# First token half four slabs ahead, table loads on SyncE: one change to a decoder trunk on one core

## The chip, the cores and the metric

The kernel runs on one core of a Trainium2 chip. It has TensorE (PE in the profile; its weight loads are PEld), VectorE (DVE), ScalarE (ACT), GpSimd (POOL) and SyncE (SP, which only starts transfers here). The metric is the device time of one execution in microseconds, as the median of several runs.

## The reference

A trunk of two post-norm layers over 256 tokens of 2048 channels in fp32. Every layer does `h = LN(a*h + mixer(h))`, then `h = LN(a*h + ffn(h))`.

```python
def reference(x, ...):
    for layer in range(DEPTH):                      # DEPTH = 2
        if layer % 2 == 0:
            mix = even_mixer(...)   # Mamba-2 SSD (16 heads) and block attention (8 heads)
        else:
            mix = odd_mixer(...)    # NSA (compressed, selected, window) and retention
        h = layer_norm(DEEPNORM_ALPHA * h + mix, ln_g[layer, 0], ln_b[layer, 0])
        ffn = conv_ffn(h, ffn_w_up[layer], ffn_conv_w[layer], ffn_conv_b[layer], ffn_w_down[layer])
        h = layer_norm(DEEPNORM_ALPHA * h + ffn, ln_g[layer, 1], ln_b[layer, 1])
def conv_ffn(x, w_up, conv_w, conv_b, w_down):
    a, u = jnp.split(x @ w_up, 2, axis=-1)
    return (jax.nn.silu(causal_depthwise_conv(a, conv_w, conv_b)) * u) @ w_down
```

Attention adds a relative-position bias, a table of 32 buckets by 8 heads. The SSD needs `dt = softplus(dt_raw + dt_bias)` before its decays.

## The kernel before

**Precision and the weight stream.** Each fp32 operand is split into a high half (rounded to the matmul's type) and a low half (the rest), and a product is made of three matmuls: high x high, high x low, low x high. All weights, some 430 MB, come once from HBM in slabs of up to 128x1024. SyncE loads a slab into `wraw` (L103), ScalarE rounds it to `whi` (L115), VectorE subtracts to `wlo` (L116); each has four buffers. `pump` splits slabs ahead of their use, `limit` bounds how far, `load` only starts transfers. With `pin` an instruction keeps its place in the program's order; the rest are ordered by the Tile scheduler when the kernel is built. On each engine the order is fixed from then on, and an engine stands at an instruction until what it needs is there.

**Jobs.** A projection is one of several kinds of jobs: `group_b` leaves channels on partitions (weights stationary, L267 and in the head L219 and L223), `group_a` and `group_t` leave tokens on partitions (`products`, L307 to L309). Tokens are two halves of 128, t = 0 and 1.

**The four LayerNorms.** `out_proj` (idx 0 to 3) makes the last projection of each half layer in four column groups of 512. In the last one the final slabs (`skew`) run first for t = 0, then for t = 1, so that the first token half ends earlier. VectorE adds it to the residual r, makes statistics (`bn_stats`, `bn_aggr`, `rs`), GpSimd raises `rs` to the power -1/2, VectorE centres the first 512 channels. `late` then calls `norm(idx, 0)`: TensorE transposes the first `SPLIT` channel blocks, ScalarE makes of each the high half `x` (L434) and the plain value y (L435, in a spare `wraw`), and VectorE the low half (`lows`, L437).

**Junctions.** After idx 0, 1 and 2 the next job begins with `SPLIT` head slabs, one channel block each (`head_slabs`): first all for t = 0, then all for t = 1. Ahead of the last one of t = 0 `ready` calls `norm(idx, 1)`, which does the same for the second token half. The other channel blocks follow, two at a time, in `norm_full`. I call these junctions 0, 1 and 2. Junctions 0 and 2 lead into an up-projection (`group_b`; `head_b` uses high weights alone for t = 0, and both high and low for t = 1). Junction 1 leads into the odd layer's `group_a` job, whose head uses high and low weights for both halves.

**The tables.** `load_bias` brings the bias, two heads at a time, from a scratch in HBM (`scr`) into `tmp` (two buffers, shared with the sums of `group_b`'s halves, L345 and L348), and VectorE copies it reversed into `nb` (L568). The even layer also loads a causal `mask`. Before, GpSimd issues these, pinned, in program order. At that place VectorE makes the softplus as a chain of small operations (L758 to L771), then `neg` (L774), which TensorE needs at L779.

Of the kernel before, what the change touches and what calls it, by code (L numbers as in the profile page):

```python
# [9 lines left out]
F32 = mybir.dt.float32  # L10
F32R = mybir.dt.float32r
AF = mybir.ActivationFunctionType
OP = mybir.AluOpType
# [5 lines left out]
KT = DM // 128  # L19
# [6 lines left out]
BIG = 1e30  # L26
NCMP = 15
AHEAD = 3
SPLIT = 3

EV_Z, EV_XS, EV_B, EV_C, EV_DT, EV_Q, EV_K, EV_V = 0, 1024, 2048, 2304, 2560, 2576, 3600, 4624
OD_Q, OD_KC, OD_VC, OD_KS, OD_VS, OD_KW, OD_VW, OD_G, OD_RQ, OD_RK, OD_RV, OD_RG = (
# [48 lines left out]
class Weights:  # L81
# [21 lines left out]
            self.nc.sync.dma_start(raw[:, :z], bass.AP(tensor=ap.tensor, offset=ap.offset + off, ap=[[z, 128], [1, z]]))  # L103
            self.raw.append(raw)

    def prep(self, i, pin=False):
        nc = self.nc
        ap, off, kind, m, width = self.slabs[i]
        n = m * width
        if not self.raw:  # L110
            self.load(i + 1)
        raw = self.raw.pop(0)
        hi = self.pool.tile([128, 1024], F32R, name="whi", bufs=4)
        lo = self.pool.tile([128, 1024], F32R, name="wlo", bufs=4)
        a = nc.scalar.activation(hi[:, :n], raw[:, :n], AF.Copy)  # L115
        b = nc.vector.tensor_tensor(lo[:, :n], raw[:, :n], hi[:, :n].bitcast(F32), op=OP.subtract)  # L116
        if pin:
            self.tc.keep_in_program_order(a)
            self.tc.keep_in_program_order(b)
        self.ready[i] = (hi[:, :n].rearrange("p (k c) -> p k c", k=m), lo[:, :n].rearrange("p (k c) -> p k c", k=m))  # L120

    def pump(self, n, pin=False):
        while self.done < min(n, len(self.slabs)):
            self.prep(self.done, pin)
            self.done += 1

    def get(self, i):
        self.pump(max(i + 1, min(i + AHEAD + 1, self.limit)))
# [39 lines left out]
class Trunk:  # L168
# [22 lines left out]
    def head_slabs(self, first, half):  # L191

        w = self.w
        n, ready = self.head
        self.head = None
        slabs = [w.get(first + i) for i in range(n)]
        for t in range(2):
            for k, (hi, lo) in enumerate(slabs):
                if t == 0 and k == n - 1:
                    ready()  # L200
                    w.pump(first + n + 1, pin=True)
                half(t, k, hi[:, 0], lo[:, 0])
                if t == 1:
                    self.apply_to(n + k + 1)
                    self.fill.pop()
        w.limit = len(w.slabs)
        return n
# [103 lines left out]
    def group_t(self, act, accs, evac, drain=None, skew=1, late=None):  # L311

        w = self.w
        first = w.first[self.job]
        self.job += 1
        m = w.slabs[first][3]  # L320
        n = act.shape[1] // m
        runs = [[s] for s in range(n - skew)] + [list(range(n - skew, n))]
        for run in runs:
            if run[0] == drain:
                self.fill.flush()
            slabs = [w.get(first + s) for s in run]
            for t in range(2):
                for s, (hi, lo) in zip(run, slabs):
                    for kk in range(m):
                        if late and t == 1 and s == n - 1 and kk == m - 1:  # L330
                            late()
                        self.products(accs[t], act, m * s + kk, t, hi[:, kk], lo[:, kk])
                        if t == 1:
                            self.fill.pop()
                if run[-1] == n - 1:
                    evac(accs[t], t)
# [16 lines left out]
    def out_proj(self, act, idx, rows=None):  # L353

        nc, r, w = self.nc, self.r, self.w
        bn = self.bn

        def evac(n):
            def go(acc, t):
                rg = r[:, t, 512 * n:512 * n + 512]  # L360
                add = nc.vector.tensor_tensor(rg, acc, rg, op=OP.add)
                if n == 3 and t == 1:
                    self.pin(add)
                    self.low()
                sums = nc.vector.bn_stats(bn[:, t, n, :], rg)
                if n < 3:
                    return
                self.pin(sums)
                self.stats(t)
                self.low()  # L370
                if idx < 3 and t == 0:
                    self.centre(0, 0, 512)
                elif idx < 3:
                    w.limit += 1
                    w.pump(w.limit, pin=True)
                else:
                    for c in range(0, DM, 512):
                        if t == 1 and c:
                            self.finish(0, c, rows)
                    for c in range(0, DM if t else 512, 512):  # L380
                        self.finish(t, c, rows)
            return go

        def late():
            self.norm(idx, 0)
            self.low()

        for n in range(4):
            if n % 2:
                accs = [self.ps() for _ in range(2)]  # L390
            else:
                accs = [self.acc_pool.tile([128, 2, 512], F32, name="acc")[:, 0, :] for _ in range(2)]
            if n == 3 and idx < 3:
                w.limit = w.first[self.job + 1] + SPLIT - 1
            self.group_t(act, accs, evac(n), drain=6 if n == 0 else None, skew=3 if n == 3 else 1,
                         late=late if n == 3 and idx < 3 else None)
        self.fill.flush()
        self.fill.rate = 1.0
        if idx < 3:
            self.applies = [(k, lambda k=k: self.norm_full(idx, k)) for k in (SPLIT, *range(SPLIT + 1, KT, 2))]  # L400
            self.head = SPLIT, lambda: self.norm(idx, 1)

    def pin(self, ins):
        return self.tc.keep_in_program_order(ins)
# [11 lines left out]
    def low(self):  # L416
        if self.lows:
            self.lows.pop(0)()

    def norm(self, idx, t):  # L420

        nc, r, x = self.nc, self.r, self.x
        if t == 0:
            self.scratch = self.w.pool.tile([128, 1024], F32, name="wraw", bufs=4)
        else:
            self.pin(self.centre(1, 0, 512))
        ps = self.ps()
        for k in range(SPLIT):
            nc.tensor.transpose(ps[:, 128 * k:128 * k + 128], r[:, t, 128 * k:128 * k + 128], self.ident)
        for k in range(SPLIT):  # L430
            g, b = self.lng[:, idx, k:k + 1], self.lnb[:, idx, k:k + 1]
            z, y = ps[:, 128 * k:128 * k + 128], self.scratch[:, 128 * (SPLIT * t + k):128 * (SPLIT * t + k) + 128]
            hi, lo = (x[:, k, 256 * i + 128 * t:256 * i + 128 * t + 128] for i in range(2))
            nc.scalar.activation(hi, z, AF.Identity, scale=g, bias=b)  # L434
            nc.scalar.activation(y, z, AF.Identity, scale=g, bias=b)  # L435
            self.lows.append(lambda lo=lo, y=y, hi=hi: self.pin(
                nc.vector.tensor_tensor(lo, y, hi.bitcast(F32), op=OP.subtract)))  # L437
        if t == 1:
            while self.lows:
                self.low()  # L440
            for half in range(2):
                self.pin(self.centre(half, 512, 512))

    def norm_full(self, idx, k0):

        nc, r, x = self.nc, self.r, self.x
        ks = [k0] if k0 == SPLIT else [k0, k0 + 1]
        ps = self.ps()
        for i, k in enumerate(ks):
            for t in range(2):  # L450
# [2 lines left out]
        for i, k in enumerate(ks):  # L453
            g, b = self.lng[:, idx, k:k + 1], self.lnb[:, idx, k:k + 1]
            z, y = ps[:, 256 * i:256 * i + 256], self.spare[:, 256 * (k % 4):256 * (k % 4) + 256]
            hi = x[:, k, :256]
# [102 lines left out]
    def load_bias(self, nb, tmp_pool):  # L559

        nc = self.nc
        self.nb = nb
        s = self.scr[:, :]
        for a in range(4):
            t = tmp_pool.tile([128, 2, 256], F32, name="tmp", bufs=2)
            self.pin(nc.gpsimd.dma_start(t, bass.AP(tensor=s.tensor, offset=s.offset + 2 * a * 384,
                                         ap=[[1, 128], [384, 2], [1, 256]])))
            nc.vector.tensor_copy(self.nb[:, 2 * a:2 * a + 2, :], t[:, :, ::-1])  # L568

    def softmax(self, P, S, nb0, nb1, w0, w1, z, stat, j):  # L570
# [94 lines left out]
    def even(self):  # L665
        nc, x = self.nc, self.x
        with ExitStack() as ctx:
            P = ctx.enter_context(self.tc.tile_pool(name="even", bufs=1))
            y = P.tile([128, KT, 512], F32R, name="y")
# [50 lines left out]
            self.zbufs = 3  # L720
            with self.tc.tile_pool(name="even2", bufs=1) as P2:
                mask = P2.tile([128, 384], F32, name="mask")
                self.pin(nc.gpsimd.dma_start(mask, self.I["c_mask"]))
                self.load_bias(P2.tile([128, H, 256], F32, name="nb"), P)
                self.fill.flush()
                self.fill.add(*self.ssd_steps(P2, y, dt, xs, bc, zs, mask))
# [4 lines left out]
                for i in range(4):  # L731
                    q = P2.tile([128, 2, 256], F32, name="q", bufs=2)
                    k = P2.tile([128, 2, 256], F32, name="k", bufs=2)
# [520 lines left out]
```

## Time and profile before

| what | value |
| --- | --- |
| median of 3 runs | 2327.4 us (2326.22 to 2328.61) |
| the profiled execution's own time | 2327.03 us |
| its span | 2325.3 us |
| TensorE busy | 2294.7 us, 99% |
| VectorE busy | 1442.3 us, 62% |
| ScalarE busy | 1133.3 us, 49% |
| GpSimd busy | 45.3 us, 2% |

The span is the time between the first and the last instruction of the profiled execution. TensorE does matmuls nearly all the time; the two engines that prepare its operands have half and a third of their time free, on average over stages that differ.

### The profile page before, as it was taken

How to read it: one execution, taken by the hardware profiler on the slowest of the kernel's cores; microseconds unless marked ns; L12 is line 12 of the kernel's file. 1: busy time of each engine (PE TensorE's matmuls, PEld its weight loads, DVE VectorE, ACT ScalarE, POOL GpSimd, SP SyncE). 2: the span in 40 equal slices, each digit the busy share in tenths (PEclk: the TensorE clock that was granted, in tenths of full speed). 3: DMA queues.
4: the chain of work that ended last, by engine and by line, in shares of the span. 5: the costliest groups of instructions: out<-in, count | busy, mean ns of one | idle time of the engine just before them, and what ended most of it. 6: DMA issues, size and time to landing. Idle time of an engine off the chain costs nothing.

```text
span 2325.3 us, 32033 instructions
## 1 busy us (share of the span) xinstructions
PE 2294.7 (99%) x12450; PEld 1975.9 (85%) x12450; DVE 1442.3 (62%) x2015; ACT 1133.3 (49%) x1501; POOL 45.3 (2%) x72
## 2 busy tenths in 40 slices
PE   8999999999999999999999999999999999999997
PEld 8888888888888888888789888888888888888885
DVE  5677656866666665444665667758766666654445
ACT  5544545655555554333545554437555555543342
POOL 0001000000000000000000000000000000000000
PEclk9999999999999999999999999999999999999998
DMA  8554444765556655666556634455655556566553
GB/s 287 193 171 154 163 166 158 228 197 189 188 190 188 191 187 192 192 193 195 183 194 221 227 109 146 154 180 191 217 190 190 189 185 189 190 222 198 194 192 125
DMA packets 124568, 436.62 MB, mean 188 GB/s; under 512 B 14176, under 2 KB 14480, under 8 KB 124288
## 3 DMA queue, kind: packets, MB, share of 16 engines
q1 hardware_dynamic: 120896, 422.58, 55.6%
q0 software_dynamic: 3520, 12.00, 1.9%
q8 instruction: 97, 1.59, 0.3%
q14 instruction: 55, 0.45, 0.1%
HBM read 432.41 MB, written 2.11 MB: 187 GB/s over the span
## 4 chain that ended last, share of the span: by engine, by line
PE 97%; DVE 1%; ACT 1%; DMA 1%; issue 0%; POOL 0%; SPq 0%; POOLq 0%; ACTq 0%; DVEq 0%
PE acc L267 57%; PE acc L308 7%; PE acc L307 7%; PE acc L309 7%; PE ps L309 5%; PE ps L307 5%; PE ps L308 5%; PE ps L659 1%; PE ps L267 1%; PE ps L598 0%; DMA tmp<-scr 0%; PE ps L451 0%; PE ps L625 0%; DVE wlo L116 0%; PE ps L597 0%
## 5 line engine op out<-in xcount | busy, mean ns | idle before, releaser
L116 DVE TENSOR_TENSOR wlo<-wraw,whi 128x1024 fp32r<-128x1024 f32 (+5 forms) x816 | 972.3, 1193 | 651.2 <-ACT whi L115 650.5
L115 ACT ACTIVATE whi<-wraw 128x1024 fp32r<-128x1024 f32 (+5 forms) x816 | 843.3, 1035 | 794.7 <-PE acc L267 288.9
L267 PE MATMUL acc<-x,whi 128*128 128x512 f32 x3816 | 1192.6, 398 | 0.0
L267 PEld LDWEIGHTS acc<-x,wlo 128*128 128x128 f32 x3816 | 700.7, 188 | 158.6 <-issue 0.2
L267 PE MATMUL acc<-x,wlo 128*128 128x256 f32 x3816 | 734.8, 279 | 0.0
L267 PEld LDWEIGHTS acc<-x,whi 128*128 128x128 f32 x3816 | 590.7, 189 | 12.5 <-issue 1.2
L345 ACT ACTIVATE tmp<-acc 128x512 f32<-128x512 f32 x120 | 71.6, 597 | 219.9 <-PE acc L267 217.3
L307 PE MATMUL ps<-whi,g 128*128 128x512 f32 x352 | 137.0, 389 | 0.0
L308 PE MATMUL acc<-wlo,g 128*128 128x512 f32 x352 | 137.0, 389 | 0.0
L309 PE MATMUL acc<-whi,g 128*128 128x512 f32 x352 | 137.0, 389 | 0.0
L308 PE MATMUL ps<-wlo,g 128*128 128x512 f32 x352 | 136.9, 389 | 0.0
L309 PE MATMUL ps<-whi,g 128*128 128x512 f32 x352 | 136.9, 389 | 0.0
L307 PE MATMUL acc<-whi,g 128*128 128x512 f32 x352 | 136.8, 390 | 0.0
L307 PE MATMUL acc<-whi,x 128*128 128x512 f32 (+4 forms) x288 | 101.1, 352 | 5.8 <-ACT whi L115 5.8
L308 PE MATMUL acc<-wlo,x 128*128 128x512 f32 (+4 forms) x288 | 100.7, 349 | 0.7 <-DVE wlo L116 0.7
L309 PE MATMUL acc<-whi,x 128*128 128x512 f32 (+4 forms) x288 | 100.1, 348 | 0.0
L307 PEld LDWEIGHTS acc<-whi,g 128*128 128x128 f32 x352 | 66.1, 188 | 14.2 <-DVE u L348 0.5
L309 PEld LDWEIGHTS acc<-whi,g 128*128 128x128 f32 x352 | 66.1, 188 | 13.8
L308 PEld LDWEIGHTS ps<-wlo,g 128*128 128x128 f32 x352 | 66.1, 188 | 13.7
L307 PEld LDWEIGHTS ps<-whi,g 128*128 128x128 f32 x352 | 66.1, 188 | 13.7
L309 PEld LDWEIGHTS ps<-whi,g 128*128 128x128 f32 x352 | 66.1, 188 | 13.7
L308 PEld LDWEIGHTS acc<-wlo,g 128*128 128x128 f32 x352 | 66.1, 188 | 13.6
(280 smaller groups left out, 1828.7 us busy)
## 6 DMA issues: line engine op xcount, KB each, us to landing
wraw<-in_up SPq DMA_DIRECT2D x328, 512.0 KB, 3.8
wraw<-in_down SPq DMA_DIRECT2D x176, 512.0 KB, 4.2
wraw<-in_od_in SPq DMA_DIRECT2D x96, 512.0 KB, 3.9
wraw<-in_ev_in SPq DMA_DIRECT2D x72, 512.0 KB, 3.6
wraw<-in_ev_out SPq DMA_DIRECT2D x32, 512.0 KB, 3.5
wraw<-in_od_out SPq DMA_DIRECT2D x32, 512.0 KB, 3.5
wraw<-in_up SPq DMA_DIRECT2D x32, 384.0 KB, 3.5
wraw<-in_ev_in SPq DMA_DIRECT2D x16, 344.0 KB, 4.4
```

The lines of the kernel that those rows point to most:

```text
L115: a = nc.scalar.activation(hi[:, :n], raw[:, :n], AF.Copy)
L116: b = nc.vector.tensor_tensor(lo[:, :n], raw[:, :n], hi[:, :n].bitcast(F32), op=OP.subtract)
L267: nc.tensor.matmul(acc, wt, mv, start=(k == 0 and i < len(unit)), stop=(k == nk - 1 and i >= len(unit)))
L307: nc.tensor.matmul(o, xh, wh, start=(k == 0), stop=False)
L308: nc.tensor.matmul(o, xh, wl, start=False, stop=False)
L309: nc.tensor.matmul(o, xl, wh, start=False, stop=(k == last))
L345: nc.scalar.activation(t, a[:, :, 256:], AF.Copy, scale=sign)
L659: nc.tensor.matmul(o[:, t * 128:(t + 1) * 128], a, b, start=(i == 0), stop=(i == len(mms) - 1))
```

## The change

- `SPLIT` becomes 4, 3, 4 for junctions 0, 1, 2; the last column group's `skew` is 4; the first half's transposes come one `kk` earlier.
- `prep` is parted: `prep_hi` does ScalarE's part and returns `rest`, VectorE's part. The last head slab is prepared in `norm(idx, 1)`, and its `rest` is called after all lows of the second half.
- For the first two blocks VectorE makes y itself, from PSUM (own name `own`), just ahead of the low.
- The mask and the four table loads go from GpSimd's queue, where they were pinned, to SyncE's, not pinned.

```diff
-SPLIT = 3
+SPLIT = (4, 3, 4)
...
-    def prep(self, i, pin=False):
+    def prep_hi(self, pin=False):
+        nc, i = self.nc, self.done
+        self.done += 1
...
         a = nc.scalar.activation(hi[:, :n], raw[:, :n], AF.Copy)
-        b = nc.vector.tensor_tensor(lo[:, :n], raw[:, :n], hi[:, :n].bitcast(F32), op=OP.subtract)
...
+        def rest():
+            b = nc.vector.tensor_tensor(lo[:, :n], raw[:, :n], hi[:, :n].bitcast(F32), op=OP.subtract)
+            if pin:
+                self.tc.keep_in_program_order(b)
+        return rest
     def pump(self, n, pin=False):
         while self.done < min(n, len(self.slabs)):
-            self.prep(self.done, pin)
-            self.done += 1
+            if not self.raw:
+                self.load(self.done + 1)
+            self.prep_hi(pin)()
...
-        slabs = [w.get(first + i) for i in range(n)]
+        slabs = [w.get(first + i) for i in range(n - 1)]
         for t in range(2):
-            for k, (hi, lo) in enumerate(slabs):
+            for k in range(n):
                 if t == 0 and k == n - 1:
+                    w.load(first + n)
                     ready()
-                    w.pump(first + n + 1, pin=True)
+                    w.limit = first + n + 1
+                    slabs.append(w.get(first + k))
+                hi, lo = slabs[k]
...
-                        if late and t == 1 and s == n - 1 and kk == m - 1:
+                        if late and t == 1 and s == n - 1 and kk == 0:
...
-                elif idx < 3:
-                    w.limit += 1
-                    w.pump(w.limit, pin=True)
-                else:
+                elif idx == 3:
...
         def late():
             self.norm(idx, 0)
             self.low()
+            self.low()
...
-            self.group_t(act, accs, evac(n), drain=6 if n == 0 else None, skew=3 if n == 3 else 1,
+            self.group_t(act, accs, evac(n), drain=6 if n == 0 else None, skew=4 if n == 3 else 1,
...
     def norm(self, idx, t):
+        n, w = SPLIT[idx], self.w
...
             self.pin(self.centre(1, 0, 512))
+            rest = w.prep_hi(pin=True)
...
-            nc.scalar.activation(hi, z, AF.Identity, scale=g, bias=b)
-            nc.scalar.activation(y, z, AF.Identity, scale=g, bias=b)
-            self.lows.append(lambda lo=lo, y=y, hi=hi: self.pin(
-                nc.vector.tensor_tensor(lo, y, hi.bitcast(F32), op=OP.subtract)))
+            self.pin(nc.scalar.activation(hi, z, AF.Identity, scale=g, bias=b))
+            if k >= 2:
+                self.pin(nc.scalar.activation(y, z, AF.Identity, scale=g, bias=b))
+            def low(lo=lo, y=y, hi=hi, z=z, g=g, b=b, own=k < 2):
+                if own:
+                    self.pin(nc.vector.tensor_scalar(y, z, g, b, op0=OP.mult, op1=OP.add))
+                self.pin(nc.vector.tensor_tensor(lo, y, hi.bitcast(F32), op=OP.subtract))
+            self.lows.append(low)
         if t == 1:
             while self.lows:
                 self.low()
+            rest()
             for half in range(2):
                 self.pin(self.centre(half, 512, 512))
...
-            self.pin(nc.gpsimd.dma_start(t, bass.AP(tensor=s.tensor, offset=s.offset + 2 * a * 384,
-                                         ap=[[1, 128], [384, 2], [1, 256]])))
+            nc.sync.dma_start(t, bass.AP(tensor=s.tensor, offset=s.offset + 2 * a * 384,
+                                         ap=[[1, 128], [384, 2], [1, 256]]))
...
-                self.pin(nc.gpsimd.dma_start(mask, self.I["c_mask"]))
+                nc.sync.dma_start(mask, self.I["c_mask"])
```

How the built order changes, at three places. Line numbers of the changed kernel are up to 16 higher than before's (L116 is L121, L437 is L450, L568 is L584).

Even layer, at the tables. GpSimd's rows of before:

```order
L723 DMA mask<-in_c_mask 128x384
L566 DMA tmp<-scr 128x2x256 x4
```

SyncE's rows of the changed kernel at that place (before, they were 72 weight loads in a row):

```order
L103 DMA wraw<-in_ev_in 128x1024 x31
L582 DMA tmp<-scr 128x2x256 x2
L103 DMA wraw<-in_ev_in 128x1024
L739 DMA mask<-in_c_mask 128x384
L103 DMA wraw<-in_ev_in 128x1024
L582 DMA tmp<-scr 128x2x256 x2
L103 DMA wraw<-in_ev_in 128x1024 x39
```

The first two table loads moved ahead of the mask, and the other two behind it, with one weight load each between.

Junction 1, VectorE. Before, from the second half's residual add (`r<-ps,r`) to the first lows of the second half (`x<-wraw,x` behind the centring `r<-r,mv,rs`):

```order
L361 TENSOR_TENSOR r<-ps,r 128x512
L437 TENSOR_TENSOR x<-wraw,x 128x128
L365 BN_STATS bn<-r 128x6
L408 BN_AGGR mv<-bn 128x2
L409 TENSOR_SCALAR rs<-mv 128x1
L437 TENSOR_TENSOR x<-wraw,x 128x128
L116 TENSOR_TENSOR wlo<-wraw,whi 128x1024
L414 TENSOR_SCALAR r<-r,mv,rs 128x512
L184 TENSOR_TENSOR y<-prm,y 128x16x2 x2
L437 TENSOR_TENSOR x<-wraw,x 128x128 x3
```

The changed kernel there, from the statistics on (`wraw<-ps,prm` is VectorE's own y, `x<-nb,x` a low of `norm_full`):

```order
L190 TENSOR_TENSOR y<-prm,y 128x16x2
L415 BN_AGGR mv<-bn 128x2
L416 TENSOR_SCALAR rs<-mv 128x1
L421 TENSOR_SCALAR r<-r,mv,rs 128x512
L449 TENSOR_SCALAR wraw<-ps,prm 128x128
L450 TENSOR_TENSOR x<-wraw,x 128x128
L449 TENSOR_SCALAR wraw<-ps,prm 128x128
L478 TENSOR_TENSOR x<-nb,x 128x256
L450 TENSOR_TENSOR x<-wraw,x 128x128 x2
L121 TENSOR_TENSOR wlo<-wraw,whi 128x1024
```

The third head slab's `wlo` moved from ahead of the centring to behind all lows of the second half and one of `norm_full`. On TensorE in the changed kernel the second half's transposes stand ahead of the first matmul that uses it:

```order
L316 MATMUL acc<-whi,x 128x512 x2
L438 MATMUL ps<-ident,r 128x128 x3
L467 MATMUL ps<-ident,r 128x128 x2
L317 MATMUL acc<-wlo,x 128x512
L318 MATMUL acc<-whi,x 128x512
```

The transposes of `norm_full` moved in front of that matmul as well; they stood behind it before.

Junction 0, VectorE. Before, from the first half's centring to its last low:

```order
L414 TENSOR_SCALAR r<-r,mv,rs 128x512
L116 TENSOR_TENSOR wlo<-wraw,whi 128x768
L437 TENSOR_TENSOR x<-wraw,x 128x128
L361 TENSOR_TENSOR r<-ps,r 128x512
L437 TENSOR_TENSOR x<-wraw,x 128x128
```

In the changed kernel:

```order
L421 TENSOR_SCALAR r<-r,mv,rs 128x512
L121 TENSOR_TENSOR wlo<-wraw,whi 128x768 x3
L449 TENSOR_SCALAR wraw<-ps,prm 128x128
L450 TENSOR_TENSOR x<-wraw,x 128x128
L449 TENSOR_SCALAR wraw<-ps,prm 128x128
L450 TENSOR_TENSOR x<-wraw,x 128x128
L370 TENSOR_TENSOR r<-ps,r 128x512
```

Two more splits stand between the centring and the first low, and two lows instead of one ahead of the second half's residual add.

## Rows read from the trace of the kernel before

**Rows 1.** Page, part 1: busy time, share of the span, instructions.
```profile
PE 2294.7 (99%) x12450; PEld 1975.9 (85%) x12450; DVE 1442.3 (62%) x2015; ACT 1133.3 (49%) x1501; POOL 45.3 (2%) x72
```

**Rows 2.** What TensorE waited for: us in total, times, longest us.
```profile
PE acc L219 <- DVE x L437: 3.9, 6, 1.0
PE ps L779 <- DVE neg L774: 3.1, 1, 3.1
PE acc L308 <- DVE wlo L116: 0.7, 2, 0.5
```

**Rows 3.** Timeline of GpSimd at the tables: start, duration, what, idle before.
```profile
129.35 1.45 POOL L566 DMA_DIRECT2D tmp<-scr  x2
134.97 1.61 POOL L566 DMA_DIRECT2D tmp<-scr  x2 [4.17 <-DMA tmp<-scr]
```

**Rows 4.** The table loads' line in the even layer, issue to landing.
```profile
DMA to landing us min/median/max: 3.5/4.7/4.9
```

**Rows 5.** Timeline of VectorE at the tables.
```profile
123.47 0.69 DVE L348 TENSOR_TENSOR pad<-acc,tmp 128x512 f32<-128x512 f32 x1 [1.29 <-ACT tmp L345]
...
127.93 1.22 DVE L116 TENSOR_TENSOR wlo<-wraw,whi 128x1024 fp32r<-128x1024 f32 x1
...
140.52 0.43 DVE L568 COPY nb<-tmp 128x512 f32<-128x512 f32 x1 [1.51 <-DMA tmp<-scr]
...
146.48 0.19 DVE L774 SCALAR_TENSOR_TENSOR neg<-dt,sp_a 128x32 f32<-128x32 f32 x1
```

**Rows 6.** Stretches behind that wait: busy by engine, PEclk, DMA share, GB/s.
```profile
148.40:151.90 3.50, 3.50 (x15) 3.17 (x15) 1.34 (x2) 0.00 (x0) 0.00 (x0) 0.51 0.80 254
151.90:156.00 4.10, 4.10 (x28) 3.66 (x28) 2.53 (x4) 2.55 (x4) 0.00 (x0) 1.00 0.10 41
```

**Rows 7.** Timeline of TensorE at junction 0.
```profile
383.96 0.74 PE L219 MATMUL acc<-x,whi 128*128 128x256 f32 x4 [0.52 <-DVE x L437]
...
386.14 0.71 PE L219 MATMUL acc<-x,whi 128*128 128x256 f32 x4 [0.41 <-DVE x L437]
...
387.39 0.55 PE L429 MATMUL ps<-ident,r 128*128 128x128 f32 x3 [0.30 <-DVE r L414]
...
389.16 0.51 PE L219 MATMUL acc<-x,whi 128*128 128x256 f32 x2 [1.00 <-DVE x L437]
```

**Rows 8.** Timeline of VectorE at junction 0.
```profile
382.05 0.95 DVE L116 TENSOR_TENSOR wlo<-wraw,whi 128x768 fp32r<-128x768 f32 x1
```

**Rows 9.** Groups by line and shape, VectorE, the SSD's masks from PSUM.
```profile
L816 DVE TENSOR_SCALAR L<-ps,acum 128x128 f32<-128x128 f32 x16 | 5.5, 341 | 0.0
```

**Rows 10.** Timeline of TensorE at junction 1.
```profile
1119.53 0.39 PE L307 MATMUL ps<-whi,g 128*128 128x512 f32 x1
...
1125.82 0.49 PE L429 MATMUL ps<-ident,r 128*128 128x128 f32 x3
...
1126.86 0.50 PE L307 MATMUL acc<-whi,x 128*128 128x512 f32 x1
```

**Rows 11.** Timeline of VectorE at junction 1.
```profile
1119.59 0.55 DVE L414 TENSOR_SCALAR r<-r,mv,rs 128x512 f32<-128x512 f32 x1 [0.68 <-POOL rs L410]
...
1121.83 0.68 DVE L361 TENSOR_TENSOR r<-ps,r 128x512 f32<-128x512 f32 x1
...
1123.65 0.15 DVE L409 TENSOR_SCALAR rs<-mv 128x1 f32<-128x1 f32 x1
...
1123.96 1.23 DVE L116 TENSOR_TENSOR wlo<-wraw,whi 128x1024 fp32r<-128x1024 f32 x1
...
1130.84 0.42 DVE L462 TENSOR_TENSOR x<-nb,x 128x256 fp32r<-128x256 f32 x1
```

**Rows 12.** Timeline of ScalarE at junction 1.
```profile
1122.85 1.08 ACT L115 ACTIVATE whi<-wraw 128x1024 fp32r<-128x1024 f32 x1
...
1126.35 0.46 ACT L434 ACTIVATE x<-ps,prm 128x128 fp32r<-128x128 f32 x1 [2.17 <-PE ps L429]
...
1129.81 0.60 ACT L459 ACTIVATE nb<-ps,prm 128x256 f32<-128x256 f32 x1
```

More of the change, by code (lines that the diff above doesn't have):

```diff
@@ L104, in load @@
             self.raw.append(raw)
-    def prep(self, i, pin=False):
-        nc = self.nc
+    def prep_hi(self, pin=False):
+        nc, i = self.nc, self.done
+        self.done += 1
         ap, off, kind, m, width = self.slabs[i]
         n = m * width
-        if not self.raw:
-            self.load(i + 1)
         raw = self.raw.pop(0)
@@ L115, in prep @@
         a = nc.scalar.activation(hi[:, :n], raw[:, :n], AF.Copy)
-        b = nc.vector.tensor_tensor(lo[:, :n], raw[:, :n], hi[:, :n].bitcast(F32), op=OP.subtract)
         if pin:
             self.tc.keep_in_program_order(a)
-            self.tc.keep_in_program_order(b)
         self.ready[i] = (hi[:, :n].rearrange("p (k c) -> p k c", k=m), lo[:, :n].rearrange("p (k c) -> p k c", k=m))
+        def rest():
[3 more added lines that the diff above has]
+        return rest
     def pump(self, n, pin=False):
         while self.done < min(n, len(self.slabs)):
-            self.prep(self.done, pin)
-            self.done += 1
+            if not self.raw:
+                self.load(self.done + 1)
+            self.prep_hi(pin)()
     def get(self, i):
@@ L393, in out_proj @@
             if n == 3 and idx < 3:
-                w.limit = w.first[self.job + 1] + SPLIT - 1
-            self.group_t(act, accs, evac(n), drain=6 if n == 0 else None, skew=3 if n == 3 else 1,
+                w.limit = w.first[self.job + 1] + SPLIT[idx] - 1
+            self.group_t(act, accs, evac(n), drain=6 if n == 0 else None, skew=4 if n == 3 else 1,
                          late=late if n == 3 and idx < 3 else None)
@@ L399, in out_proj @@
         if idx < 3:
-            self.applies = [(k, lambda k=k: self.norm_full(idx, k)) for k in (SPLIT, *range(SPLIT + 1, KT, 2))]
-            self.head = SPLIT, lambda: self.norm(idx, 1)
+            self.applies = [(k, lambda k=k: self.norm_full(idx, k)) for k in [3] * (SPLIT[idx] == 3) + list(range(4, KT, 2))]
+            self.head = SPLIT[idx], lambda: self.norm(idx, 1)
     def pin(self, ins):
@@ L422, in norm @@
         nc, r, x = self.nc, self.r, self.x
+        n, w = SPLIT[idx], self.w
         if t == 0:
-            self.scratch = self.w.pool.tile([128, 1024], F32, name="wraw", bufs=4)
+            self.scratch = w.pool.tile([128, 1024], F32, name="wraw", bufs=4)
         else:
             self.pin(self.centre(1, 0, 512))
+            rest = w.prep_hi(pin=True)
         ps = self.ps()
-        for k in range(SPLIT):
+        for k in range(n):
             nc.tensor.transpose(ps[:, 128 * k:128 * k + 128], r[:, t, 128 * k:128 * k + 128], self.ident)
-        for k in range(SPLIT):
+        for k in range(n):
             g, b = self.lng[:, idx, k:k + 1], self.lnb[:, idx, k:k + 1]
-            z, y = ps[:, 128 * k:128 * k + 128], self.scratch[:, 128 * (SPLIT * t + k):128 * (SPLIT * t + k) + 128]
+            z, y = ps[:, 128 * k:128 * k + 128], self.scratch[:, 128 * (n * t + k):128 * (n * t + k) + 128]
             hi, lo = (x[:, k, 256 * i + 128 * t:256 * i + 128 * t + 128] for i in range(2))
-            nc.scalar.activation(hi, z, AF.Identity, scale=g, bias=b)
-            nc.scalar.activation(y, z, AF.Identity, scale=g, bias=b)
-            self.lows.append(lambda lo=lo, y=y, hi=hi: self.pin(
-                nc.vector.tensor_tensor(lo, y, hi.bitcast(F32), op=OP.subtract)))
+            self.pin(nc.scalar.activation(hi, z, AF.Identity, scale=g, bias=b))
[6 more added lines that the diff above has]
+            self.lows.append(low)
         if t == 1:
@@ L446, in norm_full @@
         nc, r, x = self.nc, self.r, self.x
-        ks = [k0] if k0 == SPLIT else [k0, k0 + 1]
+        ks = [k0] if k0 == 3 else [k0, k0 + 1]
         ps = self.ps()
```

## The prediction

> **What bounds the kernel now.** The page comes first: TensorE is busy for 99% of the span [rows 1], so an edit changes the time by what it adds to or takes from TensorE's idle time, its clock, or its own work. The list of what TensorE waits for [rows 2] then shows how little there is to win: apart from the start, 3.9 us in six waits for the low halves of x (`acc L219 <- DVE x L437`, three at each of junctions 0 and 2), 3.1 us in one wait for `neg`, 0.7 us in two waits for a weight's low half (0.5 of it at junction 1). I follow each part of the change to one of these places. Times are microseconds from the span's start.
>
> **Part 1, table loads on SyncE (even layer).** TensorE stands for 3.1 us until 146.7, because `neg` is the last link of a softplus chain on VectorE that stands between the copies `nb<-tmp`. GpSimd issued the first two table loads at 129.35 and the next two only at 134.97 [rows 3]; they take 4.7 us to land [rows 4]; the last copy began at 140.52, after VectorE had idled 1.51 us for it, and `neg` began at 146.48 [rows 5]. GpSimd was late because its pinned order put the mask first, and the mask needs memory that the convolution's last step (`xs L697`) frees. With the change SP issues the first pair ahead of the mask (the order above), and these loads need only a free `tmp`, the last of which VectorE's sum at 123.47 reads until 124.2. The second pair needs the first two copies, which VectorE can do behind its split of 127.93, from 129.1 on [rows 5]; issued at about 129.7, it lands at about 134.4 in place of 140.5. I walked VectorE's new order from there with the durations of before (small steps of the chain 0.2 each, splits 1.22). `neg` ends at about 142.6. TensorE asks for it at 146.7 - 3.1 = 143.6, so the cover is about 1.0 us and the wait goes: **-3.1**. Behind the wait the granted clock fell to 0.51 for 3.5 us and was 1.00 again in the next stretch [rows 6]; at half speed that lost 0.49 x 3.5 = 1.7 us. With no wait there is no reason for it: **-1.7**. Bounds: nothing, if the wait only moves, to -4.8. I take **-4.8**, since the walk leaves a margin. What is queued behind the five DMAs on SP is the weight stream. The two loads that they stand in front of waited for VectorE anyhow and go out at their old time or up to 3 us earlier. In the odd layer four loads move as well; there no row of TensorE waits for anything, and I count **0** (0 to +0.5, if a weight load of one of these slabs is held up by the copy that a table load waits for).
>
> **Part 2, junctions 0 and 2 (four slabs).** TensorE's rows show the first head matmul starting at 383.96 after a wait, the next waits ending at 386.14 and, for the transposes, 387.39, and the second token half at 389.16 [rows 7]. The idle times in the rows (0.52, 0.41, 0.30, 1.00) count from a matmul's end; a matmul lasts 0.40 there and the next can start 0.23 after its start, so each is 0.17 to 0.2 more in lateness: 0.7, 0.6, 0.5 and 1.2, 3.0 us for a junction. The fourth slab gives the first half one more slab of cover, and the transposes come one `kk` earlier. But the order now puts three `wlo` splits (0.95 us each [rows 8]) ahead of the first low of x, where one stood before; the third can't start before ScalarE has split a slab whose buffer the out-projection frees late. My walk gives waits of 0.8 at the first slab, 0.4 at the fourth (its low stands behind the residual add and the statistics), 0.5 at the transposes, 0.8 at the second half, and a new one of 0.7 at the first full transposes: 3.2, and six more short matmuls cost under 0.1. So **+0.2 each, +0.4 together**. Bounds: -1.3 each if the third split doesn't hold up the lows, +0.8 each if ScalarE's part comes later than I put it. The value y that VectorE now makes from PSUM costs it 0.34 (the nearest row: the same operation, 128x128 from PSUM [rows 9]) and takes as much from ScalarE; it is in the walk.
>
> **Part 3, junction 1 (three slabs, and the low weight split last).** This is where I see the loss. Before, TensorE waited 0.5 once, for `wlo` [rows 2], and the second half's first matmul came at 1126.86 [rows 10]. There the head's job uses low weights in the first token half too. Before, the third slab's `wlo` was split at 1123.96, right after the statistics and ahead of the centring [rows 11]. After, it stands on VectorE behind the centring, y0, its low, y1, a low of `norm_full`, and two more lows (the order above), and TensorE, in program order, stands at the third slab's first `acc<-wlo,x`. Step by step:
> - First-half transposes at 1119.53, where the last out-projection slab begins its second half [rows 10]. ScalarE then makes three hi, one y and the third slab's `whi` (1.08 [rows 12]), and only then the `y<-prm` piece for which VectorE now waits ahead of its second low. So the residual add of the second half starts at about 1123.1 in place of 1121.83.
> - From that add to `rs` took 1.82 (1121.83 to 1123.65), from `rs` over GpSimd to the centring 0.83 (0.15 + 0.68 [rows 11]), and the centring 0.55: transposes at about 1126.3. TensorE has done its last out-projection slab and two head slabs (18 matmuls and 2 at 0.23 each, 0.4 of transposes) and wants them at about 1119.53 + 5.0 = 1124.5. **Wait 1.8.** Before they came at 1125.82, but behind work that could go ahead.
> - From the transposes on: hi0 after 0.57; then ScalarE does two more hi, a y, a 256-wide x and a 256-wide `nb`, at 0.35 to 0.60 each [rows 12], so `nb` is there 3.0 after the transposes. VectorE's 256-wide low (0.42), two lows (0.2 of pitch each) and the split (1.23) [rows 11] end at 5.1. TensorE has 0.5 of transposes to do in that time. **Wait 4.5.**
> - Four matmuls (0.94) later, at about 1132.3, the second half begins, 5.3 to 5.5 after the 1126.86 of before, with the same work behind it. Nothing later was waiting, so nothing takes it back: **+5.3**.
> - The clock: TensorE is idle for about 6.3 of 6.8 us here, twice what the wait for `neg` was, and that cost 0.49 x 3.5 us of clock afterwards [rows 6]. I take the same again: **+1.7**; bounds 0 (the shorter waits of the junctions are followed by a clock of 1.00) and 3.4 (two such stretches).
> The Trainium skill, "TensorE: Matmul & The Clock Gate", Part 1, says that the throttled state is the default and that activity releases it; by it a dip behind a stall of this kind is to be expected, and by the short waits' rows alone the sum would be 1.7 lower. The stretch at 0.51 behind the 3.1 us agrees with the page.
> Bounds of the part: +0.5 if the split is in fact done before the transposes, +8.7 with two stretches. I take +7.0, as every link of it is in the built order.
>
> **Sum.** The profiled execution took 2327.0 (span 2325.3 and 1.7 around it); the median is 2327.4, 0.4 above. 2327.0 - 4.8 + 0 + 0.4 + 5.3 + 1.7 = 2329.6, and against the median **2330.0**. A measurement of this kernel tells 0.2% from no change, that is 4.7 us: faster is below 2322.7, slower above 2332.1.
>
> **Rivals.**
> - *The stall at junction 1 is small.* For it: if VectorE's split were done ahead of the lows as before, only 0.5 of wait stood there; and the fourth slab was worth 1.3 at each of the other junctions by the lower bound. Against it: the built order has the split behind `x<-nb`. Time: 2327.4 - 4.8 + 0.5 - 0 to 2.6 = 2320.5 to 2323.1. Chance 0.14.
> - *The wait for `neg` stays (the other sign).* The place is the same ps L779. The second pair of tables could land later on SP, behind the weight loads and with the 16 engines at a 0.60 share there, and the copies stand in the middle of the chain. Its price: for every us beyond the 1.0 of cover TensorE waits as long, and the half-clock stretch returns with it. From 0.4 us of wait plus the 1.7 of clock on, the sum passes 2332.1; with all of the old wait it is 2327.4 + 0.4 + 7.0 = 2334.8. For it: the landing times spread from 3.5 to 4.9 [rows 4]. Against: the walk has the tables 6 us earlier than before. Chance 0.15.
> - *SP holds up the weight stream.* A table load that waits for VectorE's copy stops every weight load behind it. For it: SP waits in order. Against: the slabs in question are split well before TensorE needs them. From 1 us of lateness beyond that cover it costs as much as it is late, at two places: 2331 to 2334. Chance 0.05.
> - *The clock falls twice behind the stall* (+1.7): 2331.7, inside my range, still no difference that can be told. It is in the forecast's case.
>
> **How the numbers follow.** Forecast, all in all 0.66: its own range is 2328.0 to 2332.0. With the rivals' parts beyond the two limits: faster 0.12, within 0.2% 0.66, slower 0.22. The range that leaves out at most two in ten reaches into both sides: 2323.0 to 2333.8.
>
> **What the changed kernel's profile would show.** Right: no wait for `neg`, and a clock of 1.00 from 147 to 152; at junction 1 one wait of 4 to 5 us of `acc<-wlo,x` for VectorE's `wlo` and one of 1 to 2 us of the transposes for r, and a stretch of half clock behind them; at junctions 0 and 2 waits that sum to 2.5 to 3.8 each. Wrong: no long wait for `wlo` at junction 1 (then the step on VectorE's order failed), a wait for `neg` of over 0.5 us (then the walk at the tables did), or waits under 2 us at junctions 0 and 2.

## The result and the profile after

The changed kernel takes **2340.5 us** (median of 4 runs, 2340.0 to 2341.7) against 2327.7 for the kernel before in the same runs: a ratio of 1.0056, interval 1.0041 to 1.0071. It is slower by some 13 us; the forecast was 2330.0, with a range of 2323.0 to 2333.8. The profiled execution took 2341.7, its span is 2339.9, 14.6 more than before.

The changed kernel's list of what TensorE waits for (us in total, times, longest):

```profile
PE acc L228 <- DVE x L450: 6.5, 4, 2.9
PE acc L316 <- ACT whi L115: 6.2, 1, 6.2
PE acc L317 <- DVE wlo L121: 4.6, 2, 4.3
PE acc L228 <- ACT whi L115: 4.1, 2, 2.1
PE ps L438 <- DVE r L421: 1.7, 3, 1.3
PE ps L795 <- DVE neg L790: 0.5, 1, 0.5
```

Against [rows 2]: the wait for `neg` fell from 3.1 to 0.5 (forecast: gone); the wait for `wlo` at junction 1 rose from 0.5 to 4.3 (forecast: 4.5). But the waits at the first matmuls of junctions 0 and 2 rose from 3.9 in six to 10.6 in six (6.5 and 4.1; what the 2.1 really were is shown below). The 6.2 are the start, 5.8 before.

To place the difference I take one instruction in both traces, the nth of ScalarE's 816 weight splits, and how much later it starts than before. These are its rows on ScalarE's timeline of the changed kernel for n = 51, 121, 151, 391, 421:

```profile
120.15 1.06 ACT L115 ACTIVATE whi<-wraw 128x1024 fp32r<-128x1024 f32 x1 [1.40 <-issue]
...
349.36 1.06 ACT L115 ACTIVATE whi<-wraw 128x1024 fp32r<-128x1024 f32 x1 [1.66 <-PE acc L318]
...
433.86 1.04 ACT L115 ACTIVATE whi<-wraw 128x1024 fp32r<-128x1024 f32 x1
...
1098.18 1.06 ACT L115 ACTIVATE whi<-wraw 128x1024 fp32r<-128x1024 f32 x1 [1.66 <-PE ps L318]
...
1192.79 1.06 ACT L115 ACTIVATE whi<-wraw 128x1024 fp32r<-128x1024 f32 x1 [1.66 <-PE acc L318]
```

Before, the same ones started at 119.86, 353.18, 432.25, 1096.61 and 1183.48:

```profile
353.18 1.06 ACT L115 ACTIVATE whi<-wraw 128x1024 fp32r<-128x1024 f32 x1 [1.66 <-PE acc L309]
...
432.25 1.04 ACT L115 ACTIVATE whi<-wraw 128x1024 fp32r<-128x1024 f32 x1
...
1183.48 1.06 ACT L115 ACTIVATE whi<-wraw 128x1024 fp32r<-128x1024 f32 x1 [1.66 <-PE acc L309]
```

The differences are +0.3, -3.8, +1.6, +1.6 and +9.3; just ahead of junction 2 it is +9.4 (the 541st) and behind it +14.7 (1649.76 for 1635.05, the 576th). So by stage, with the same made for the experiments' profiled executions:

| kernel | start | tables | junction 0 | junction 1 | junction 2 |
| --- | --- | --- | --- | --- | --- |
| changed | +0.3 | -4.1 | +5.4 | +7.7 | +5.3 |
| forecast | 0 | -4.8 | +0.2 | +7.0 | +0.2 |
| e1_tables_sp | +0.3 | -4.9 | +1.5 | +0.1 | 0.0 |
| e1_again (same kernel) | -1.2 | -4.9 | 0.0 | 0.0 | 0.0 |
| e2_y_scalar | +0.3 | -4.4 | -0.6 | +4.8 | -0.6 |
| e3_two_banks | -0.6 | -4.9 | +0.3 | +6.2 | +0.3 |
| e4_split_first | -0.8 | -4.9 | +5.4 | +1.2 | +4.7 |
| e5_best | -0.5 | -3.9 | -0.6 | +0.1 | -0.6 |
| e6_three | -0.5 | -4.9 | +0.9 | +0.1 | -0.4 |
| e7_keep_busy | -0.5 | -4.7 | +3.3 | +6.6 | +3.3 |

The start differs from execution to execution by up to 1.5 us (the two rows of the same kernel) and belongs to no edit; between the stages the differences are some 0.1 or less. The tables and junction 1 came near the forecast; junctions 0 and 2 lost 5.4 and 5.3 where 0.2 was expected.

Junction 0 in the changed kernel, first TensorE's timeline (its waits), then VectorE's and ScalarE's:

```profile
377.72 0.60 PE L438 MATMUL ps<-ident,r 128*128 128x128 f32 x4
...
381.77 0.71 PE L228 MATMUL acc<-x,whi 128*128 128x256 f32 x4 [2.05 <-ACT whi L115]
...
385.44 0.66 PE L438 MATMUL ps<-ident,r 128*128 128x128 f32 x4 [0.22 <-DVE r L421]
...
389.25 0.76 PE L228 MATMUL acc<-x,whi 128*128 128x256 f32 x2 [2.92 <-DVE x L450]
```

```profile
376.87 2.89 DVE L121 TENSOR_TENSOR wlo<-wraw,whi 128x768 fp32r<-128x768 f32 x3
380.89 0.41 DVE L449 TENSOR_SCALAR wraw<-ps,prm 128x128 f32<-128x128 f32 x1 [1.13 <-ACT wraw L445]
381.34 0.29 DVE L450 TENSOR_TENSOR x<-wraw,x 128x128 fp32r<-128x128 f32 x1
...
388.37 0.41 DVE L449 TENSOR_SCALAR wraw<-ps,prm 128x128 f32<-128x128 f32 x1 [2.99 <-ACT wraw L445]
388.81 0.29 DVE L450 TENSOR_TENSOR x<-wraw,x 128x128 fp32r<-128x128 f32 x1
```

```profile
378.67 1.14 ACT L443 ACTIVATE x<-ps,prm 128x128 fp32r<-128x128 f32 x3
379.70 0.46 ACT L445 ACTIVATE wraw<-ps,prm 128x128 f32<-128x128 f32 x1
380.04 0.47 ACT L443 ACTIVATE x<-ps,prm 128x128 fp32r<-128x128 f32 x1
380.38 0.47 ACT L445 ACTIVATE wraw<-ps,prm 128x128 f32<-128x128 f32 x1
380.91 0.84 ACT L115 ACTIVATE whi<-wraw 128x768 fp32r<-128x768 f32 x1
```

VectorE's own y (L449) needs the transposed block alone, which was there before 378.67, when ScalarE began to read it; VectorE was free from 379.76. It begins at 380.89, when ScalarE's *last* y (block 3, 380.38 + 0.47) is done, and again at 388.37 in the second half, after 2.99 us of idle time. The low then ends at 381.63, and the matmul at 381.77 follows it. The row calls ScalarE's split of 380.91 the releaser, since that ended last, at 381.75; in the built program this matmul waits for the low and for ScalarE's *first* high half, which was long done. The experiment with two tiles below shows that it doesn't wait for that split: there the same matmul starts at 378.86 and ScalarE's split at 379.22. A releaser in such a row is the one that ended last by time, and has to be checked where its data make no sense.

At junction 1 the long wait is the forecast one, of `acc<-wlo,x` for VectorE's split:

```profile
1132.90 0.79 PE L317 MATMUL acc<-wlo,x 128*128 128x512 f32 x1 [4.34 <-DVE wlo L121]
```

The clock, by windows of the changed kernel (busy of PE, PEld, DVE, ACT, POOL, then PEclk, DMA share, GB/s):

```profile
148.00:152.00 4.00, 4.00 (x27) 3.56 (x26) 2.34 (x3) 2.30 (x4) 0.00 (x0) 1.00 0.51 155
379.00:387.80 8.80, 4.71 (x32) 3.69 (x30) 4.64 (x12) 4.37 (x12) 0.55 (x1) 0.99 0.39 130
387.80:394.60 6.80, 5.35 (x26) 5.38 (x27) 4.46 (x10) 1.45 (x4) 0.00 (x0) 0.51 0.39 119
394.70:400.00 5.30, 5.30 (x42) 5.08 (x41) 4.53 (x9) 4.87 (x9) 0.00 (x0) 1.00 0.45 144
1131.90:1138.70 6.80, 5.80 (x14) 4.57 (x15) 3.03 (x5) 1.06 (x1) 0.00 (x0) 0.51 0.69 230
1589.50:1595.90 6.40, 4.96 (x23) 5.00 (x24) 4.46 (x10) 1.36 (x3) 0.00 (x0) 0.50 0.38 122
```

At each of the three stalls TensorE's clock fell to 1.2 instead of 2.4 GHz, for about twice as long as behind the wait for `neg` in [rows 6]. The Trainium skill, "TensorE: Matmul & The Clock Gate", Part 1, says that activity releases the throttle. The rows at junction 0 agree: 0.51 from 387.80 on, where TensorE is still idle at first, and 1.00 from 394.70 on, after work.

### The profile page after: what moved, and what is told of

Its sections match the earlier page's. It is cut to its first block, busy times and chain, and to the rows that moved or that the text cites. A ratio compares the mean times of both kernels' runs of the same rounds, so it can differ in the third digit from the quotient of the medians.

```text
span 2339.9 us, 32081 instructions
## 1 busy us (share of the span) xinstructions
PE 2299.7 (98%) x12462; PEld 1981.7 (85%) x12462; DVE 1446.6 (62%) x2029; ACT 1130.4 (48%) x1493; POOL 38.9 (2%) x63
## 4 chain that ended last, share of the span: by engine, by line
PE 96%; DVE 2%; issue 1%; ACT 1%; DMA 0%; POOL 0%; SPq 0%; ACTq 0%; POOLq 0%; DVEq 0%
PE acc L276 56%; PE acc L317 7%; PE acc L318 7%; PE acc L316 7%; PE ps L318 4%; PE ps L317 4%; PE ps L316 4%; PE ps L675 1%; PE ps L276 1%; PE ps L614 0%; DVE wlo L121 0%; PE ps L467 0%; PE ps L641 0%; PE ps L613 0%; PE acc L228 0%
## 5 line engine op out<-in xcount | busy, mean ns | idle before, releaser
L121 DVE TENSOR_TENSOR wlo<-wraw,whi 128x1024 fp32r<-128x1024 f32 (+5 forms) x816 | 972.4, 1193 | 658.5 <-ACT whi L115 657.7
```

## The experiments

Theory, after the result: at junctions 0 and 2 VectorE's y waits until ScalarE has read all of the transposed tile, as both read the same PSUM tile; that idles TensorE for some 3 us more at each of the two, and the clock falls with it. At junction 1 the late split of the low weights is the cause, as forecast. Rivals: the three weight splits ahead of the first low; the spare buffer that both engines write; the clock as a bystander.

**The tables alone.** The kernel before with only this edit (in the even layer `mask`, in both layers `tmp`):

```diff
-            self.pin(nc.gpsimd.dma_start(t, bass.AP(...)))
+            nc.sync.dma_start(t, bass.AP(...))
-                self.pin(nc.gpsimd.dma_start(mask, self.I["c_mask"]))
+                nc.sync.dma_start(mask, self.I["c_mask"])
```

> The kernel before with one part of the change: mask and table loads issued by SyncE. Theory: the change's stage up to 160 us became 4.1 us shorter (3.1 to 0.5 us of wait for neg, and the half-clock stretch behind it gone), and that is this part's doing alone: 2327.7 - 4.1 = 2323.6. Rival: the weight stream behind the moved loads is held up in the odd layer, or the gain needs other parts of the change: 2325.5 to 2328.

Measured: 2321.6, before 2328.4, ratio 0.997 (0.9958 to 0.9982), 2 us below the theory. The stage gave -4.9 and the odd layer nothing (within 0.1). The medians differ by 6.8, which is 1.9 more than the stage: the profiled execution of before, with which the stages are compared, lies 1.4 below the median of before in these runs (2327.0 for 2328.4), and 0.5 is not placed. VectorE's timeline there shows what the walk in the prediction described, and one wait that it did not name:

```profile
129.40 0.76 DVE L568 COPY nb<-tmp 128x512 f32<-128x512 f32 x2
...
131.50 1.02 DVE L790 TENSOR_TENSOR cbm<-ps,mask 128x384 f32<-128x384 f32 x2 [0.81 <-DMA mask<-in_c_mask]
...
134.37 0.42 DVE L568 COPY nb<-tmp 128x512 f32<-128x512 f32 x1
...
135.93 0.42 DVE L568 COPY nb<-tmp 128x512 f32<-128x512 f32 x1
...
142.33 0.19 DVE L774 SCALAR_TENSOR_TENSOR neg<-dt,sp_a 128x32 f32<-128x32 f32 x1
```

The walk had the second pair of tables at 134.4 and the end of `neg` at 142.6. In the changed kernel the third copy began at 136.28 and `neg` at 144.24, which left 0.5 us of wait and is why it got 4.1. What made the difference is the mask, whose product stands ahead of the third copy on VectorE; the copy itself starts without a wait:

```profile
133.40 1.02 DVE L806 TENSOR_TENSOR cbm<-ps,mask 128x384 f32<-128x384 f32 x2 [2.76 <-DMA mask<-in_c_mask]
...
136.28 0.42 DVE L584 COPY nb<-tmp 128x512 f32<-128x512 f32 x1
```

Both kernels issue the mask at 128.4, but VectorE stood for it 2.76 us here and 0.81 there, 1.9 apart, as the third copies are. The other runs agree: TensorE waited for `neg` only where VectorE idled longer than 2.2 us ahead of this product (2.42, 2.76 and 2.94 us of idle time, 0.2, 0.5 and 0.7 of wait), and these are the stage's -4.4, -4.1 and -3.9. Run on another occasion, the same kernel confirmed the stage's -4.9:

> The kernel before with the tables on SyncE once more, on the same chip as the kernel with both repairs, to see which of the two is faster. Theory: 0 to 1.5 us faster than that kernel (2321.5 to 2322), since at junction 1 it keeps the order of before. Rival: the two repairs leave the fourth slab's gain, and it is 0.5 us or more slower.

Measured: 2321.6 beside 2327.9, ratio 0.9976 (0.9967 to 0.9985). That is 0.8 above the kernel with both repairs (below), where 0 to 1.5 less was expected; the intervals of the two overlap.

**ScalarE makes every y.**

```diff
-            if k >= 2:
+            if True:
                 self.pin(nc.scalar.activation(y, z, AF.Identity, scale=g, bias=b))
-            def low(lo=lo, y=y, hi=hi, z=z, g=g, b=b, own=k < 2):
+            def low(lo=lo, y=y, hi=hi, z=z, g=g, b=b, own=False):
```

> The changed kernel with ScalarE making every plain value y again, each right behind its high half. Theory: the loss of 5.4 us at each of junctions 0 and 2 comes from VectorE's own y, which waits until ScalarE has read the whole transposed tile; without it the first low is there 1.7 us sooner at the first slab and 1.8 us sooner at the second half, and the idle time no longer pulls the clock down (2.7 us): 2 x 6.2 less, some 2328. Rival: the three weight splits that stand ahead of the first low are the cause; then at most 1 us a junction comes back: 2338 to 2340.

Measured: 2326.4, ratio to before 0.9991 (0.9982 to 0.9999): 14 us less than the changed kernel. At junction 0 +5.4 became -0.6, the clock stayed at full speed there, and the three splits ahead of the first low were still in place, so they weren't the cause. The same edit took junction 1 from +7.7 to +4.8: its waits are 0.4 and 3.5 there instead of 1.3 and 4.3. TensorE's waits at junction 0 in this kernel, and the window around them:

```profile
379.67 0.74 PE L228 MATMUL acc<-x,whi 128*128 128x256 f32 x4 [0.30 <-DVE x L450]
382.38 0.47 PE L228 MATMUL acc<-x,whi 128*128 128x256 f32 x2 [0.29 <-DVE x L450]
383.30 0.66 PE L438 MATMUL ps<-ident,r 128*128 128x128 f32 x4 [0.46 <-DVE r L421]
385.18 0.50 PE L228 MATMUL acc<-x,whi 128*128 128x256 f32 x2 [0.75 <-DVE x L450]
```

```profile
375.00:400.00 25.00, 23.22 (x154) 20.56 (x153) 20.40 (x41) 18.53 (x36) 1.10 (x2) 1.00 0.49 158
```

**Two tiles for the transposes.** VectorE keeps its y, but blocks 0 and 1 have a PSUM tile of their own:

```diff
-        ps = self.ps()
+        ps, two = self.ps(), self.ps()
         for k in range(n):
-            nc.tensor.transpose(ps[:, ...], r[:, t, 128 * k:128 * k + 128], self.ident)
+            nc.tensor.transpose((two if k < 2 else ps)[:, ...], r[:, t, 128 * k:128 * k + 128], self.ident)
...
-            z, y = ps[:, ...], self.scratch[:, ...]
+            z, y = (two if k < 2 else ps)[:, ...], self.scratch[:, ...]
```

> The changed kernel, but the first two blocks are transposed into a PSUM tile of their own. Theory: VectorE's y waits for ScalarE's last read of the tile that it reads; now that is the second high half and no longer the last y, so the first low comes 1.2 us sooner for the first token half and 1.5 us sooner for the second, at junctions 0 and 2: 5.4 us less of idle, and as much of clock if it no longer falls: 2329.5 to 2335. Rival: the wait is for ScalarE's writes to the spare weight buffer that holds all y; then nothing changes, 2340.5.

Measured: 2328.2, ratio to before 1.0000 (0.9991 to 1.0008): 12 us less than the changed kernel, and 1.3 below the theory's range, in a kernel where all y still share the spare buffer. So the shared PSUM tile is what VectorE's y waits for. On VectorE's timeline the first half's y now begins with no wait, and the second half's at ScalarE's second high half:

```profile
377.99 0.40 DVE L449 TENSOR_SCALAR wraw<-ps,prm 128x128 f32<-128x128 f32 x1
...
383.84 0.41 DVE L449 TENSOR_SCALAR wraw<-ps,prm 128x128 f32<-128x128 f32 x1 [1.37 <-ACT x L443]
```

**The low split first at junction 1.**

```diff
             rest = w.prep_hi(pin=True)
+            if idx == 1:
+                rest()
...
-            rest()
+            if idx != 1:
+                rest()
```

> The changed kernel, but at junction 1 the third slab's low weights are split right behind the centring, ahead of the lows. Theory: the 4.3 us wait there is for that split; it shrinks to under 1 us and another 0.8 us appears at the first low of the second half, and the clock stays up: 5 to 6 us less, 2334.5 to 2335.5. Rival: the lows then come later by what the split takes, and the gain is 3 us or less: 2337.5 to 2340.

Measured: 2334.0, ratio to before 1.0022 (1.0012 to 1.0032), 6.5 less than the changed kernel and 0.5 below the theory's range; the 0.8 us that the theory expected at the second half's first low did not appear. Junction 1 went from +7.7 to +1.2; its waits are now these, with a clock of 1.00 behind them:

```profile
PE ps L440 <- DVE r L421: 1.3, 1, 1.3
PE acc L317 <- DVE wlo L121: 0.4, 1, 0.4
```

**TensorE kept at work.** The changed kernel with transposes of the identity that nobody reads, 16 ahead of the first head slab and 26 ahead of the second token half, at junctions 0 and 2:

```diff
         for t in range(2):
+            if n == 4:
+                idle = self.ps()
+                for _ in range(26 if t else 16):
+                    self.pin(nc.tensor.transpose(idle[:, :128], self.ident, self.ident))
             for k in range(n):
```

> The changed kernel with idle transposes (128x128, of the identity, read by nobody) on TensorE at junctions 0 and 2: 16 ahead of the first head slab, 26 ahead of the second token half, where it waits. They take about as long as the waits, so the waits' length is hardly changed, but TensorE is not idle. Theory: of the 5.4 us lost at each of the two junctions some 2.5 are the clock's, which falls to half behind the waits; with TensorE at work it stays up: 5 us less, 2335 to 2336.5. Rival: the clock's fall costs little since the matmuls behind it wait for other engines anyhow: within 1.5 us of 2340.5, or more.

Measured: 2336.2, ratio to before 1.0035 (1.0022 to 1.0047): 4.3 less than the changed kernel, with more work on TensorE. The timeline shows the second filler, and the windows a full clock where it was 0.51:

```profile
384.86 3.00 PE L207 MATMUL ps<-ident 128*128 128x128 f32 x26
```

```profile
376.00:386.00 10.00, 9.13 (x68) 8.09 (x67) 6.21 (x14) 5.05 (x13) 0.55 (x1) 1.00 0.37 120
386.00:396.00 10.00, 9.92 (x81) 9.36 (x79) 7.91 (x18) 6.52 (x13) 0.00 (x0) 1.00 0.41 119
```

Junctions 0 and 2 went from 5.4 and 5.3 to 3.3 each, and the second half's first matmul still comes 3.4 us after the last head matmuls ahead of it (384.54 to 387.94 here, 385.85 to 389.25 in the changed kernel), so the wait itself is as long. Hence 2.1 of the 5.4 are the clock's and the other 3.3 the waits'. At junction 1, which had no filler, the half clock and most of the loss stayed (+6.6).

**Both repairs, and three slabs.** The changed kernel with the edits of e2 and e4; and the same with `SPLIT = (3, 3, 3)`.

> The changed kernel with both repairs: ScalarE makes every y, and at junction 1 the third slab's low weights are split ahead of the lows. Theory: the parts add up: the tables' 4.9 us less, 0.6 less at each of junctions 0 and 2 as with the first repair, and at junction 1 what is left with the second (1.2 more) or a little less: 2322.5 to 2323.5. Rival: the repairs share what they win at junction 1 (with ScalarE's y there the split was still waited for), or a half-clock stretch comes back somewhere: 2324 to 2326.

Measured: 2320.9, ratio to before 0.9970 (0.9959 to 0.9982), the lowest median of all. The granted clock is 1.00 around the tables and all three junctions (110 to 160, 370 to 400, 1100 to 1140, 1565 to 1600), and no wait of TensorE is over 0.8 us behind the start. The repairs add up, and at junction 1 nothing is left to lose (+0.1, where the theory kept up to 1.2); the median is 1.6 us below the theory's range.

> As the kernel with both repairs, but three head slabs at all junctions, so that it tells what the fourth slab is worth. Theory: with three slabs one split less stands ahead of the first low, but the second half's transposes have one slab of work less to hide behind; 0.5 to 1.3 us more at each of junctions 0 and 2: 2323.5 to 2326. Rival: the fourth slab brings nothing: within 0.5 us of the kernel with four.

Measured: 2321.2, ratio 0.9972 (0.9961 to 0.9983). The difference from the kernel with four slabs, 0.3 us, lies within the two intervals: that the fourth slab is worth something wasn't shown, and the rival came (within 0.5), not the theory. In the profiled execution there was a half-clock stretch at junction 0 (a granted clock of 0.79 from 382 to 390), where it has +0.9; at junction 2, with none, it has -0.4. Nor can these two be told from the tables alone (2321.6).

## Why the prediction was wrong

**Part 1 held in the main.** -4.8 was forecast, the changed kernel got -4.1 and the same edit alone -4.9. The mechanism was right, and the half-clock stretch behind the wait went with it (1.00 from 148 to 152). But the prediction names no wait of VectorE for the mask, which now lands behind the first pair of tables; in the changed kernel that put the third copy 1.9 us later than the walk had it, and the wait of 0.52 us for `neg` is just over the 0.5 that it called a sign of a wrong walk. SP's weight stream was not held up, and the odd layer's four loads cost nothing, as taken.

**Part 3 held.** +7.0 was forecast, +7.7 came. The two waits were 1.3 and 4.3 where 1.8 and 4.5 stood. The clock fell as assumed, but for about twice as long as behind `neg`: 0.49 x the 5.8 us of work in the window from 1131.90 is 2.8 (an estimate from that row), where 1.7 stood. Waits that were 0.7 shorter (5.6 for 6.3) and a clock that was 1.1 dearer nearly cancel, so that the sum came this close is partly luck. The experiment that moved the split confirmed the cause: it gave back 6.5 us.

**Part 2 failed, in one sentence:** "The value y that VectorE now makes from PSUM costs it 0.34 [...] and takes as much from ScalarE; it is in the walk." I had counted its duration and not its wait. In the walk VectorE's y could begin as soon as the tile was transposed and VectorE was free; in the built program it waits for ScalarE's last read of that tile. So a change that was to take work off ScalarE put ScalarE's whole list (four high halves and two y) ahead of the first low, where only one high half and one y had stood. The walk's waits of 0.8 and 0.8 at the first slab and the second half came out as 2.05 and 2.92 in the rows, 0.2 more each as the prediction counts lateness; its three others (0.4, 0.5 and 0.7) came out as 0.34, 0.22 and none. With this y given back to ScalarE the rest of the walk was on the safe side: waits of 0.30, 0.29, 0.46 and 0.75 (e2), and -0.6 a junction where I had +0.2.

**What the failed step also cost.** I looked for a fall of the clock at junction 1 alone. Stalls of 2 to 3 us at the others brought it too, and that is 2.1 us of each 5.4. My bound of +0.8 held for neither junction. Two junctions x 5.2 of error, 0.7 at junction 1 and 0.7 at the tables are 11.8, against 12.1 between the sum's 2329.6 and the profiled execution's 2341.7; the start has the other 0.3. The medians are 10.5 from the forecast, as the profiled execution was the slowest of the four.

**The rivals.** The wait for `neg` did not stay; the stall at junction 1 was not small; SP did not hold up the stream. The clock did fall for twice as long behind the stall at junction 1, as the fourth has it, which alone would have stayed inside the range. The changed kernel is slower, the side that I gave 0.22, but the miss at junctions 0 and 2 comes from none of the mechanisms that I had put there.

## What to carry to other kernels

When work moves from one engine to another, count what the receiving instruction must wait for, not only how long it takes. Here the second reader of a PSUM tile was made to wait for all reads that the first engine had ahead of it in program order; a tile of its own, or leaving both readings on one engine, was worth 5 to 6 us a place. That wait stands in the built program, and could have been read there beforehand. And where TensorE is the bound, price a stall of some microseconds with the half-clock stretch that may follow: here it added two thirds to the waits' own cost.

## What the runs showed that I had not expected

- The same short waits brought a half-clock stretch in one execution and none in another. The two profiled executions of the kernel with the tables alone have the same four waits at junction 0 (0.5, 0.4, 0.3 and 1.0 us); in the first the granted clock of a window behind them is 0.79 and junction 0 costs 1.5 us more than before, in the second it is 1.00 from 370 to 400 us and costs nothing. The window of the first:

```profile
384.00:392.00 8.00, 7.41 (x46) 7.28 (x47) 5.97 (x12) 6.93 (x14) 0.00 (x0) 0.79 0.55 170
```

And of the second:

```profile
370.00:387.00 17.00, 14.77 (x90) 12.42 (x89) 11.02 (x24) 8.89 (x19) 1.10 (x2) 1.00 0.29 94
387.00:400.00 13.00, 13.00 (x84) 11.60 (x82) 11.40 (x20) 9.14 (x16) 0.00 (x0) 1.00 0.70 213
```

The long waits at junction 1 show the same in the changed kernel and in the one with the fillers: they are 1.3 and 4.3 in both, the stage costs 7.7 in one and 6.6 in the other, and these are the 10 us behind the wait, in that order:

```profile
1132.90:1142.90 10.00, 10.00 (x34) 8.04 (x35) 5.51 (x8) 4.43 (x6) 0.00 (x0) 0.72 0.61 209
```

```profile
1129.50:1139.50 10.00, 10.00 (x40) 8.10 (x41) 6.66 (x11) 4.44 (x6) 0.00 (x0) 0.84 0.66 216
```

So what a stage costs by the clock can differ while its waits stay the same, and one profiled execution doesn't price that. What decides it was not tested here.

- Transposes that nobody reads (26 in 3.00 us) kept the clock at 1.00 over a stall that otherwise halved it, and the kernel became faster by doing more.
